# A two-table dense stage: the last token tile's weights kept in two parts, the first of which is given back at key 80

## The chip, the cores and the metric

The kernel runs on one core of a Trainium2 chip. The metric is device time of one execution in microseconds (us). Engines are named as the profile names them: PE multiplies matrices, ACT (ScalarE) copies and evaluates functions, DVE (VectorE) and POOL (GpSimd) work elementwise, SP issues most DMAs, POOL issues the indirect ones (gathers).

## The reference

Two transformer blocks over 512 tokens of width 1024, then a final norm. The change lies in the last part of the second block, a PEER layer: each token picks, for 8 heads, 16 of 128 x 128 experts, each of them one row of a table u and one row of a table v.

```python
def chunk(xc):
    ...
    eidx = jnp.take_along_axis(cidx, pos, axis=-1)
    g = jax.nn.softmax(best, axis=-1)
    a = jnp.einsum('chkd,cd->chk', u_tab[eidx], xc)
    wgt = (jax.nn.gelu(a.astype(jnp.float32)) * g).astype(xc.dtype)
    return jnp.einsum('chk,chkd->cd', wgt, v_tab[eidx])
```

## The kernel before

The function `peer` holds the layer. The tokens stand in four tiles of 128. Three of them (384 tokens, `TD`) are computed densely: for every one of the 128 first keys (here "a key", 128 experts) the kernel multiplies all tokens by the u chunk, takes gelu, multiplies by the tokens' weights for these experts (zero for experts not picked) and multiplies the result by the v chunk, all 128 keys summed in PSUM (`yp`). The fourth tile is computed sparsely: 128 gathers of u rows and 128 of v rows (`grow`), one expert of each of the 128 tokens at a time, with the products made on DVE (`gy` sums the v rows).

Each f32 chunk of a table (128 x 1024, 512 KB) is split for PE into a high and a low half: `wload` loads it into `wraw` (4 buffers, shared by all loads), ACT copies the high half (L69: `whi`, or `vhi`), DVE subtracts (L70: `wlo`, `vlo`). A product takes three matmuls (L87 to L89).

Stages around the change:

- *Weight build* (L1800 on): for each of the three tiles and 32 groups of four tokens, DVE makes one-hot matrices, PE multiplies them into a PSUM bank, and ACT evicts the bank into `gs` (L1820), a tile of 128 x 128 keys x 128 tokens, 64 KB a partition. Between the groups, first-table chunks of keys below 80 (`AHEAD`) and u gathers are worked off. After tiles 0 and 1 `gs` is stored to HBM in four parts (`gd`); tile 2's weights stay in SBUF.
- *Dense stage, keys 0 to 79*: the first-table results lie in HBM (`ad`) and are loaded. `v_prep` loads the other tiles' weights (`gw`), loads and splits the v chunk (a pool `vs` of its own with two buffers each of `vhi` and `vlo`, except for keys 0 to 3, 126 and 127), POOL multiplies weights and gelu (L1851 for two tiles, L1852 for the third out of `gs`), ACT and DVE split the product (`wah`, `wal`), and `v_mm` issues 18 matmuls into `yp`.
- *Dense stage, keys 80 to 123*: in addition `u_chunk` of the next key: load, split, 24 matmuls into `acc`, gelu on ACT (L1596, `ga`).
- Keys 124 to 127 and the final norm.

After each key `gather` is called with a count so that all 256 gathers are out by key 121: 80 are made before the dense stage, 59 in keys 0 to 79, 117 in keys 80 to 121, two or three a key. A gather takes a `grow` buffer (4 of them); right after it `use(lag)` works off rows until only `lag` are outstanding, 3 in the dense stage.

Order: POOL's instructions, and DVE's in the loop over keys, run in the order of the program text. The other engines' orders, SP's too, are fixed at build time by the framework's own estimate of when things become ready. Every engine and queue then runs its list strictly in order. A buffer's next user waits for the last reader of the one before; a pool opened where a closed one lay waits for the readers of the tiles that it covers.

Of the kernel before, what the change touches and what calls it, by code (L numbers as in the profile page):

```python
# [9 lines left out]
F32 = mybir.dt.float32  # L10
# [5 lines left out]
AF = mybir.ActivationFunctionType  # L16
ALU = mybir.AluOpType
# [4 lines left out]
D = 1024  # L22
# [24 lines left out]
class Emit:  # L47
# [1514 lines left out]
    def peer(self):  # L1562
        tc, nc, A = self.tc, self.nc, self.A
# [5 lines left out]
        gd = [tc.dram_tile([ND - 1, 128, 32, 128], F32, name=f"gd{j}") for j in range(4)]  # L1569
        ad = tc.dram_tile([AHEAD, 128, TD], F32, name="ad")  # L1570
        xd = tc.dram_tile([S, D], F32, name="xd")
        with ExitStack() as es:
# [15 lines left out]
            def u_chunk(c, eng=None):  # L1588

                wh, wl = self.wload(A["puT"][c], eng=eng)  # L1590
                p = self.acc()
                for k in range(KD):
                    s_ = slice(k * 128, k * 128 + 128)
                    self.mm3(p[:, :TD], wh[:, s_], wl[:, s_], hh[:, k, :TD], hl[:, k, :TD], k == 0, k == KD - 1)
                g = dn.tile([128, TD], F32, name="ga", bufs=4)
                nc.scalar.activation(g, p[:, :TD], AF.Gelu_apprx_tanh)  # L1596
                if c < AHEAD:
                    self.dma(ad[c], g)
                    return None
                return g  # L1600

            def ahead(n, eng=nc.gpsimd):
                for _ in range(n):
                    if nu[0] < AHEAD:
                        u_chunk(nu[0], eng)
                        nu[0] += 1
# [28 lines left out]
            ga = es.enter_context(tc.tile_pool(name="gat", bufs=4, side="right"))  # L1635
            er = es.enter_context(ExitStack())
# [2 lines left out]

            es.enter_context(tc.manual_schedule(engines={mybir.EngineType.Pool}))  # L1640

            ng, rows = [0], []

            def gather(n, lag=2):


                for _ in range(n):
                    i = ng[0]
                    if i == 256:
                        return  # L1650
                    ng[0] += 1
                    s = i % 128
                    if i == 128:
                        use(0)
                        self.dma(ht, A["g_fin"].to_broadcast([128, D]))
                        nc.scalar.activation(wt, at, AF.Gelu_apprx_tanh)
                        nc.gpsimd.tensor_tensor(wt, wt, gg, op=ALU.mult)
                    r = ga.tile([128, D], F32, name="grow")
                    nc.gpsimd.indirect_dma_start(out=r, out_offset=None, in_=A["pu" if i < 128 else "pvr"],  # L1659
                                                 in_offset=bass.IndirectOffsetOnAxis(ap=ei[:, s:s + 1], axis=0))  # L1660
                    rows.append((i, r))
                    use(lag)

            def use(lag):
                while len(rows) > lag:
                    i, r = rows.pop(0)
                    s = i % 128
                    if i < GPOOL:
                        nc.gpsimd.tensor_tensor(r, r, ht, op=ALU.mult)
                        nc.scalar.activation(r, r, AF.Copy, accum_out=at[:, s:s + 1])  # L1670
                    elif i < 128:
                        stt(r, r, 1.0, ht, op0=ALU.mult, op1=ALU.mult, accum_out=at[:, s:s + 1])  # L1672
                    elif s == 0:
                        ts(gy, r, wt[:, 0:1], None, op0=ALU.mult)
                    else:
                        stt(gy, r, wt[:, s:s + 1], gy, op0=ALU.mult, op1=ALU.add)  # L1676
# [3 lines left out]
            with ExitStack() as ek:  # L1680
# [98 lines left out]
                for t in range(ND):  # L1779
                    c = slice(t * 32, t * 32 + 32)  # L1780
                    p = self.bank()
# [9 lines left out]

            ev = es.enter_context(ExitStack())
            pg = ev.enter_context(tc.tile_pool(name="pg", bufs=1))
            gs = pg.tile([128, 128, 128], F32, name="gs")
            with ExitStack() as ek:
                p2 = ek.enter_context(tc.tile_pool(name="pg2", bufs=2))
                spare = self.wr.rearrange("p k e -> p (k e)")
                i1 = spare[:, 0:128]
                nc.gpsimd.iota(i1, pattern=[[1, 128]], base=0, channel_multiplier=0,
                               allow_small_or_imprecise_dtypes=True)  # L1800
                ih = spare[:, 128:192].bitcast(F16).rearrange("p (a b) -> p a b", b=2)
                nc.vector.tensor_copy(spare[:, 128:192].bitcast(F16), i1)
                nu0, ng0 = nu[0], ng[0]
                for t in range(ND):
                    for q in range(32):

                        e = eT[:, t * 32 + q].rearrange("p j n i -> p (j n) i")
                        o = p2.tile([128, 8, 64, 2], F16, name="oh", bufs=3)
                        tt(o, ih[:, None].to_broadcast([128, 8, 64, 2]),
                           e[:, 0:8, None].to_broadcast([128, 8, 64, 2]), op=ALU.is_equal)  # L1810
                        w = p2.tile([128, 8, 64, 2], F16, name="ohw", bufs=3)
                        for j in range(2):
                            tt(w[:, 4 * j:4 * j + 4], o[:, 4:8],  # L1813
                               e[:, 8 + 4 * j:12 + 4 * j, None].to_broadcast([128, 4, 64, 2]), op=ALU.mult)
                        p = self.bank()
                        for i in range(4):
                            for j in range(2):
                                mm(p[:, i * 128:i * 128 + 128], lhsT=o[:, i].rearrange("p a b -> p (a b)"),  # L1818
                                   rhs=w[:, 4 * j + i].rearrange("p a b -> p (a b)"), start=j == 0, stop=j == 1)
                        nc.scalar.activation(gs[:, :, q * 4:q * 4 + 4], p.rearrange("p (t e) -> p e t", t=4), AF.Copy,  # L1820
                                             scale=1.0 / WSCALE)
                        n = 32 * t + q + 1
                        ahead(nu0 + (AHEAD - nu0) * n // (32 * ND) - nu[0], None)
                        gather(ng0 + GH * n // (32 * ND) - ng[0], 3)
                    if t < ND - 1:
                        for j in range(4):
                            self.dma(gd[j][t], gs[:, j * 32:j * 32 + 32])
                ahead(AHEAD)

            er.close()  # L1830
            vs = ev.enter_context(tc.tile_pool(name="vs", bufs=2))
            eb.close()
            py = es.enter_context(tc.tile_pool(name="py", bufs=1, space=PSUM))
            yp = [py.tile([128, 512], F32, name=f"yp{i}") for i in range(2 * ND)]
            TG = TD - 128

            def v_prep(c, g, ah=None, al=None):

                if g is None:
                    g = dn.tile([128, TD], F32, name="ga", bufs=4)  # L1840
                    self.dma(g, ad[c])
                gw = dn.tile([128, TD], F32, name="gw", bufs=4)
                self.dma(gw[:, :TG], gd[c // 32][:, :, c % 32].rearrange("t a n -> a t n"))
                if c < 4 or c >= 126:
                    wh, wl = self.wload(A["pv"][c])
                else:
                    w = self.wraw.tile([128, 1024], F32, name="wraw")
                    self.dma(w, A["pv"][c])
                    wh, wl = vs.tile([128, 1024], F32R, name="vhi"), vs.tile([128, 1024], F32R, name="vlo")
                    self.split(wh, wl, w)  # L1850
                nc.gpsimd.tensor_tensor(gw[:, :TG], gw[:, :TG], g[:, :TG], op=ALU.mult)  # L1851
                nc.gpsimd.tensor_tensor(gw[:, TG:], gs[:, c], g[:, TG:], op=ALU.mult)  # L1852
                if ah is None:
                    ah, al = dn.tile([128, TD], F32R, name="wah"), dn.tile([128, TD], F32R, name="wal")
                self.split(ah, al, gw)
                return c, ah, al, wh, wl
# [11 lines left out]
            em.enter_context(tc.manual_schedule(engines={mybir.EngineType.DVE}))  # L1868
            g = None
            for c in range(124):  # L1870
                ng_ = u_chunk(c + 1) if AHEAD <= c + 1 < 128 else None
                v = v_prep(c, g)
                for t in range(ND):
                    v_mm(v, t)
                g = ng_
                if c < AHEAD:
                    m = 256 - left + n0 * (c + 1) // AHEAD
                else:
                    m = 256 - left + n0 + (left - n0) * min(c + 1 - AHEAD, GLAST - AHEAD) // (GLAST - AHEAD)
                gather(m - ng[0], 3)  # L1880
            use(0)

            gl = [g] + [u_chunk(c) for c in (125, 126, 127)]
# [43 lines left out]
AHEAD = 80  # L1927
# [15 lines left out]
WSCALE = 2.0 ** 14  # L1943
# [169 lines left out]
```

## Time and profile before

| what | us |
|---|---|
| median of 3 runs (lowest, highest) | 2685.59 (2677.74, 2690.04) |
| the profiled execution | 2691.68 |
| its span, first to last instruction | 2689.6 |
| busy: PE, DVE, ACT, POOL | 2435.8, 1819.5, 1084.8, 940.5 |

The profile is of one execution; times in its rows count from the span's start. In a row of the timeline or of the groups, the text in brackets or behind the bar is the idle time of the engine before the instruction and what ended it. The weight build lies at about 1607 to 1895 us, keys 0 to 79 end at about 2236, key 123 begins at 2636.61.

### The profile page before, as it was taken

Reading aid. Unit: us, or ns where it says so; the run is one execution under the profiler, and the core shown is the slowest. Engines: PE = TensorE matmul, PEld = TensorE weight load, DVE = VectorE, ACT = ScalarE, POOL = GpSimd, SP = SyncE. Lnnn points to the kernel's source line nnn. Section 1 sums busy time; section 2 is a strip of 40 time slices with the busy share of each in tenths; the row PEclk is TensorE's granted clock in tenths of the full one; section 3 lists DMA queues with packets and bytes.
Section 4 is the critical chain, followed back from the end, with each engine's and each line's share of the span. In section 5 each row is a group of like instructions: output and inputs, shape, how many; then the busy total and the mean of one; then the engine's idle time right before and its main releaser. Section 6 shows DMA issues by size and latency. Waiting matters only on the chain. (4 is left out here: it accounts for less than half of the span.)

```text
span 2689.6 us, 33407 instructions
## 1 busy us (share of the span) xinstructions
PE 2435.8 (91%) x11697; PEld 1904.9 (71%) x11697; DVE 1819.5 (68%) x3150; ACT 1084.8 (40%) x1697; POOL 940.5 (35%) x781
## 2 busy tenths in 40 slices
PE   7999888899969978899898989999999999999997
PEld 6776566334427756678687779988788878888886
DVE  6677975364435665654458899977777766767676
ACT  5455434232234235653435554434333333333233
POOL 1001640121100310000056664411677665656661
PEclk9999998899989988999899999999899999999999
DMA  3114675899983311124234459996699987888884
GB/s 144 56 62 155 227 279 206 314 367 409 402 315 115 94 55 32 44 75 156 83 128 135 148 175 329 350 351 248 221 307 302 305 289 256 288 273 298 273 299 139
DMA packets 214782, 585.28 MB, mean 218 GB/s; under 512 B 30437, under 2 KB 85221, under 8 KB 213588
## 3 DMA queue, kind: packets, MB, share of 16 engines
q1 hardware_dynamic: 169684, 429.71, 45.5%
q0 software_dynamic: 44928, 153.42, 16.2%
q8 instruction: 92, 1.51, 0.2%
q14 instruction: 78, 0.64, 0.1%
HBM read 537.65 MB, written 53.78 MB: 220 GB/s over the span
## 5 line engine op out<-in xcount | busy, mean ns | idle before, releaser
L69 ACT ACTIVATE whi<-wraw 128x1024 fp32r<-128x1024 f32 (+1 forms) x280 | 289.1, 1033 | 511.7 <-PE acc L88 191.9
L87 PE MATMUL acc<-hph,whi 128*128 128x384 f32 (+1 forms) x1152 | 404.8, 352 | 23.4 <-ACT ga L1596 21.8
L89 PE MATMUL acc<-hph,wlo 128*128 128x384 f32 (+1 forms) x1152 | 402.7, 350 | 11.4 <-DVE wlo L70 8.2
L88 PE MATMUL acc<-hpl,whi 128*128 128x384 f32 (+1 forms) x1152 | 399.6, 347 | 0.0
L70 DVE TENSOR_TENSOR wlo<-wraw,whi 128x1024 fp32r<-128x1024 f32 (+1 forms) x236 | 288.5, 1223 | 159.1 <-ACT whi L69 157.5
L87 PE MATMUL yp<-vhi,wah 128*128 128x512 f32 x732 | 231.7, 396 | 20.3 <-ACT wah L69 20.3
L87 PEld LDWEIGHTS acc<-hph,whi 128*128 128x128 f32 x1152 | 220.5, 192 | 35.4 <-ACT ga L1596 26.3
L89 PEld LDWEIGHTS acc<-hph,wlo 128*128 128x128 f32 x1152 | 220.2, 191 | 25.1 <-DVE wlo L70 15.3
L88 PE MATMUL yp<-vlo,wah 128*128 128x512 f32 x732 | 231.4, 395 | 0.0
L89 PE MATMUL yp<-vhi,wal 128*128 128x512 f32 x732 | 228.2, 395 | 0.0
L88 PEld LDWEIGHTS acc<-hpl,whi 128*128 128x128 f32 x1152 | 220.6, 191 | 7.5 <-DVE hpl L70 0.5
L1851 POOL TENSOR_TENSOR gw<-gw,ga 128x256 f32<-128x256 f32 x128 | 172.3, 1346 | 147.8 <-DMA ga<-ad 77.2
L1659 POOL DMA_INDIRECT grow<-pu,ei x128 | 150.9, 1179 | 206.5 <-DVE grow L1672 170.5
L70 DVE TENSOR_TENSOR vlo<-wraw,vhi 128x1024 fp32r<-128x1024 f32 x122 | 160.1, 1312 | 92.9 <-ACT vhi L69 92.8
L1659 POOL DMA_INDIRECT grow<-pvr,ei x128 | 173.2, 1353 | 123.5 <-DVE gy L1676 95.1
L69 ACT ACTIVATE wah<-gw 128x384 fp32r<-128x384 f32 x126 | 66.0, 524 | 279.4 <-POOL gw L1852 223.0
L87 PEld LDWEIGHTS yp<-vhi,wah 128*128 128x128 f32 x732 | 139.7, 191 | 52.0 <-ACT wah L69 24.1
L1676 DVE SCALAR_TENSOR_TENSOR gy<-grow,wt,gy 128x1024 f32<-128x1024 f32 x127 | 164.0, 1291 | 16.2 <-DMA grow<-pvr,ei 14.1
L70 DVE TENSOR_TENSOR wal<-gw,wah 128x384 fp32r<-128x384 f32 x126 | 93.8, 745 | 114.9 <-ACT wah L69 114.8
L89 PEld LDWEIGHTS yp<-vhi,wal 128*128 128x128 f32 x732 | 139.2, 190 | 31.7 <-DVE wal L70 2.4
L88 PEld LDWEIGHTS yp<-vlo,wah 128*128 128x128 f32 x732 | 139.8, 191 | 28.2
L70 POOL TENSOR_TENSOR wlo<-wraw,whi 128x1024 fp32r<-128x1024 f32 x44 | 106.1, 2416 | 152.5 <-ACT whi L69 139.2
(702 smaller groups left out, 5178.9 us busy)
## 6 DMA issues: line engine op xcount, KB each, us to landing
wraw<-wgu SPq DMA_DIRECT2D x128, 512.0 KB
wraw<-puT SPq DMA_DIRECT2D x128, 512.0 KB
wraw<-pv SPq DMA_DIRECT2D x128, 512.0 KB
wraw<-wd SPq DMA_DIRECT2D x64, 512.0 KB
aw<-wada SPq DMA_DIRECT2D x48, 512.0 KB
gd<-gs SPq DMA_DIRECT2D x8, 2048.0 KB
gw<-gd SPq DMA_DIRECT2D x128, 128.0 KB
ad<-ga SPq DMA_DIRECT2D x80, 192.0 KB
```

The source lines that it names most:

```text
L69: nc.scalar.activation(hi, src, AF.Copy)
L70: (eng or nc.vector).tensor_tensor(lo, src, f32(hi), op=ALU.subtract)
L87: mm(ps, lhsT=wh, rhs=xh, start=first, stop=False)
L88: mm(ps, lhsT=wh, rhs=xl, start=False, stop=False)
L89: mm(ps, lhsT=wl, rhs=xh, start=False, stop=last)
L1659: nc.gpsimd.indirect_dma_start(out=r, out_offset=None, in_=A["pu" if i < 128 else "pvr"], in_offset=bass.IndirectOffsetOnAxis(ap=ei[:, s:s ...
L1676: stt(gy, r, wt[:, s:s + 1], gy, op0=ALU.mult, op1=ALU.add)
L1851: nc.gpsimd.tensor_tensor(gw[:, :TG], gw[:, :TG], g[:, :TG], op=ALU.mult)
```

## The change

`gs` becomes two tiles: `ga_` with keys 0 to 79 (40 KB a partition, on the right side of SBUF, in the pool group `er`) and `gb` with keys 80 to 127 (24 KB). Each eviction becomes two instructions, and the stores of tiles 0 and 1 are cut at key 80. At key 80 `er` is closed, and a new pool `vs` is opened in its place, with three buffers `vraw` for loads of the second table, two of `vhi` and of `vlo`, and three more row buffers `grow2`; from then on the lag is 6, and three of each seven rows go to `grow2`. Keys below 80 take the shared `wload`.

```diff
-            ng, rows = [0], []
+            ng, rows, more = [0], [], []
...
-                    r = ga.tile([128, D], F32, name="grow")
+                    r = more[0].tile([128, D], F32, name="grow2", bufs=3) if more and (i - more[1]) % 7 < 3 else \
+                        ga.tile([128, D], F32, name="grow")
...
-            gs = pg.tile([128, 128, 128], F32, name="gs")
+            gb = pg.tile([128, 128 - AHEAD, 128], F32, name="gsb")
+            ga_ = er.enter_context(tc.tile_pool(name="pga", bufs=1, side="right")).tile([128, AHEAD, 128], F32, name="gsa")
+            gsp = (ga_, 0, AHEAD), (gb, AHEAD, 128)
...
-                        nc.scalar.activation(gs[:, :, q * 4:q * 4 + 4], p.rearrange("p (t e) -> p e t", t=4), AF.Copy,
-                                             scale=1.0 / WSCALE)
+                        pe = p.rearrange("p (t e) -> p e t", t=4)
+                        for g_, lo, up in gsp:
+                            nc.scalar.activation(g_[:, :, q * 4:q * 4 + 4], pe[:, lo:up], AF.Copy, scale=1.0 / WSCALE)
...
-                            self.dma(gd[j][t], gs[:, j * 32:j * 32 + 32])
+                            for g_, lo, up in gsp:
+                                lo_, up_ = max(lo, j * 32), min(up, j * 32 + 32)
+                                if lo_ < up_:
+                                    self.dma(gd[j][t][:, lo_ - j * 32:up_ - j * 32], g_[:, lo_ - lo:up_ - lo])
...
-            er.close()
-            vs = ev.enter_context(tc.tile_pool(name="vs", bufs=2))
+            vs = None
...
-                if c < 4 or c >= 126:
+                if c < AHEAD or c >= 126:
                     wh, wl = self.wload(A["pv"][c])
                 else:
-                    w = self.wraw.tile([128, 1024], F32, name="wraw")
+                    w = vs.tile([128, 1024], F32, name="vraw", bufs=3)
...
-                nc.gpsimd.tensor_tensor(gw[:, TG:], gs[:, c], g[:, TG:], op=ALU.mult)
+                gt = ga_[:, c] if c < AHEAD else gb[:, c - AHEAD]
+                nc.gpsimd.tensor_tensor(gw[:, TG:], gt, g[:, TG:], op=ALU.mult)
...
             for c in range(124):
+                if c == AHEAD:
+                    er.close()
+                    vs = ev.enter_context(tc.tile_pool(name="vs", bufs=2, side="right"))
+                    more += [vs, ng[0]]
...
-                gather(m - ng[0], 3)
+                gather(m - ng[0], 6 if more else 3)
```

## Rows read from the trace of the kernel before

**Rows 1.** Windows: us; busy PE, PEld, DVE, ACT, POOL (count); clock, DMA share, GB/s.

```profile
1607.00:1895.00 288.00, 270.41 (x1947) 251.47 (x1947) 253.30 (x460) 125.13 (x201) 101.43 (x65) 0.95 0.83 302
1950.00:2150.00 200.00, 200.00 (x884) 165.65 (x883) 147.59 (x171) 75.21 (x98) 141.84 (x135) 1.00 0.92 305
2277.47:2636.61 359.14, 336.91 (x1639) 297.38 (x1638) 247.95 (x223) 112.70 (x156) 220.76 (x183) 0.98 0.83 285
```

**Rows 2.** Timeline of PE (start, us, instruction, idle before): first matmuls of second-table passes.

```profile
2232.00 0.50 PE L87 MATMUL yp<-vhi,wah 128*128 128x512 f32 x1 [0.43 <-ACT wah L69]
...
2277.47 0.39 PE L87 MATMUL yp<-vhi,wah 128*128 128x512 f32 x1
...
2285.78 0.39 PE L87 MATMUL yp<-vhi,wah 128*128 128x512 f32 x1
...
2319.56 0.39 PE L87 MATMUL yp<-vhi,wah 128*128 128x512 f32 x1
...
2331.93 0.79 PE L87 MATMUL yp<-vhi,wah 128*128 128x512 f32 x1 [3.92 <-ACT wah L69]
...
2636.61 0.50 PE L87 MATMUL yp<-vhi,wah 128*128 128x512 f32 x1 [0.50 <-ACT wah L69]
```

**Rows 3.** Waits, 2277.47 to 2636.61: us in total, times, longest.

```profile
ACT whi L69 <- DMA wraw<-puT: 148.9, 39, 7.7
...
POOL gw L1851 <- issue: 38.2, 28, 9.3
...
PE yp L87 <- ACT wah L69: 15.5, 7, 3.9
DVE gy L1676 <- DMA grow<-pvr,ei: 13.0, 16, 1.6
...
PE acc L89 <- DVE wlo L70: 6.0, 11, 1.3
```

**Rows 4.** Timeline of DVE, SP and ACT, key 90.

```profile
2322.24 1.22 DVE L70 TENSOR_TENSOR wlo<-wraw,whi 128x1024 fp32r<-128x1024 f32 x1
...
2323.49 0.33 SPq L55 DMA_DIRECT2D wraw<-puT  x1
...
2330.41 1.06 ACT L69 ACTIVATE whi<-wraw 128x1024 fp32r<-128x1024 f32 x1 [7.66 <-DMA wraw<-puT]
2331.37 0.51 ACT L69 ACTIVATE wah<-gw 128x384 fp32r<-128x384 f32 x1
```

**Rows 5.** Timeline of DVE, remainders (wal) that bound keys 83 and 88.

```profile
2267.96 0.56 DVE L70 TENSOR_TENSOR wal<-gw,wah 128x384 fp32r<-128x384 f32 x1 [0.91 <-ACT wah L69]
...
2276.09 0.56 DVE L70 TENSOR_TENSOR wal<-gw,wah 128x384 fp32r<-128x384 f32 x1 [0.91 <-ACT wah L69]
...
2310.01 0.56 DVE L70 TENSOR_TENSOR wal<-gw,wah 128x384 fp32r<-128x384 f32 x1 [1.61 <-ACT wah L69]
...
2319.25 0.56 DVE L70 TENSOR_TENSOR wal<-gw,wah 128x384 fp32r<-128x384 f32 x1 [2.58 <-ACT wah L69]
```

**Rows 6.** Timeline of DVE after key 123; waits of PE from 2636 us.

```profile
2637.07 3.92 DVE L1676 SCALAR_TENSOR_TENSOR gy<-grow,wt,gy 128x1024 f32<-128x1024 f32 x3
...
PE yp L87 <- ACT hph L69: 4.0, 1, 4.0
```

**Rows 7.** Timeline of POOL at key 79.

```profile
2230.25 0.72 POOL L1851 TENSOR_TENSOR gw<-gw,ga 128x256 f32<-128x256 f32 x1 [11.32 <-DMA ga<-ad]
2230.94 0.46 POOL L1852 TENSOR_TENSOR gw<-gs,ga 128x128 f32<-128x128 f32 x1
```

**Rows 8.** Groups by shape of ACT in the weight build: count, busy, mean ns, idle before.

```profile
L1820 ACT ACTIVATE gs<-bank 128x512 f32<-128x512 f32 x96 | 53.7, 606 | 58.6 <-PE bank L1818 39.5 <-DMA gd<-gs 13.2 <-issue 5.4
L69 ACT ACTIVATE whi<-wraw 128x1024 fp32r<-128x1024 f32 x50 | 53.3, 1067 | 101.7 <-PE acc L88 101.6
L1596 ACT ACTIVATE ga<-acc 128x384 f32<-128x384 f32 x50 | 23.9, 478 | 4.8 <-issue 4.8
```

**Rows 9.** Timeline of ACT at the end of the build's first tile.

```profile
1771.02 4.03 ACT L1820 ACTIVATE gs<-bank 128x512 f32<-128x512 f32 x8 [13.16 <-DMA gd<-gs]
```

## The prediction

> **What bounds the kernel now.** I read the windows by stage first: they show for each stretch whether PE is full. From 1950 to 2150, within the first 80 keys of the dense stage, PE is busy 200.00 of 200 us, so nothing that helps other engines can pay there. In the stretch from key 84 to key 123 it is busy 336.91 of 359.14 us at a granted clock of 0.98, with the DMA engines at 0.83 [rows 1]. That stretch is where both tables are multiplied in each key, and only there is something to win.
>
> How much, the timeline of PE says. A key there is 24 matmuls of the first table and 18 of the second. Where PE waits for nothing, the second-table pass of key 84 begins at 2277.47 and that of key 85 at 2285.78: 8.31 us. Over the five keys to 2319.56 it is 8.42 us each. From 2277.47 to key 123 at 2636.61 it is 359.14/39 = 9.21 us [rows 2]. So 0.90 us a key, 35 us in all, lie above the bare PE time.
>
> Then the waits of that stretch, to see what takes it: PE waits 15.5 us for the high half of the weights (wah, ACT) and 6.0 us for the low half of a first-table chunk (DVE); the rest is matmuls at the lower clock level after such pauses, 336.91 - 39 x 8.31 = 12.8 us [rows 1, 3]. Behind them stands ACT, which waits 148.9 us for the load of the first table, 39 times, longest 7.7 us [rows 3]. Key 90 shows the mechanism: ACT has the copy of a later first-table chunk ahead of wah in its order; that chunk's load was issued at 2323.49, right behind the DVE subtraction that freed its buffer (2322.24 + 1.22), and came 6.9 us later; wah, whose input was long ready, ran at 2331.37, and PE started at 2331.93 [rows 2, 4]. The load is late because its buffer is: four wraw buffers serve two loads a key, so a load can only be issued two keys ahead of its use.
>
> **The change part by part.**
>
> 1. Loads of the second table from key 80 get three buffers of their own; the four wraw buffers serve the first table alone. A first-table load then follows the subtraction of four keys before, not two: two keys, 16.8 us at 8.42, earlier than the 6.9 us that key 90's load took [rows 2, 4]. A second-table load follows the one of three keys before. I take ACT's 148.9 us to fall to nearly nothing, and with them the late wah. POOL's multiply waits 38.2 us in 28 pieces for nothing that the profile names ("issue") [rows 3]; it needs the gelu of the chunk, which ACT makes behind the late copy, so I count these with them.
> What is late next: the loop DVE to POOL to ACT to DVE. POOL issues a key's second gather only when DVE has used up the row that sat in its buffer, the weight multiplies stand behind the gathers on POOL, wah behind them, and DVE's own next step behind wah. This coupling stays: with seven buffers and a lag of six, the buffer that a gather needs is still freed by the use emitted just before it. Its length without a late load is 8.13 us at key 83 (2267.96 to 2276.09, three rows) [rows 5], under PE's 8.31. So PE sets the pace. Ends: 8.31 (no waits, as in the first 80 keys) and 9.21 (nothing gained). I take 8.42, the five clean keys, as they have the same work: (9.21 - 8.42) x 39 = -30.8 us.
>
> 2. Three more row buffers and a lag of six. DVE waits 13.0 us in 16 waits for rows that have not landed [rows 3]; with two keys more of flight time these go. They lie inside the 9.21 and are not counted again. At the end six rows instead of three are left for DVE: 3 x 1.31 = 3.9 us, from the three at 2637.07 [rows 6]. PE then still has most of two passes to do; a wait of 4.0 us for ACT in the tail may shrink with earlier loads [rows 6]. Ends -4.0 and +3.9; I take +1.
>
> 3. Keys below 80 split their weights into the shared ring of three instead of a ring of two. PE is full there, 200.00 of 200 us [rows 1], and hides it: 0. Without that cover a third buffer could only shorten waits of ACT, so the sign would be a gain.
>
> 4. The hand-over at key 80. The new pool lies on the first part, so the second-table load of key 80 stands on SP until POOL has done its multiply of key 79 (2230.94 + 0.46), and the loads behind it on SP stand too; DVE's and ACT's work of key 80 waits for it. From there: 6.9 us of load, 1.06 of copy, 1.22 of subtraction [rows 4, 7], 9.2 us. PE has meanwhile wah and its remainder (about 1.1), the second-table pass of key 79 and a first-table pass, together 8.31: 9.4 us. So just hidden. Now the five keys from 2232.00 to 2277.47 take 45.47 us [rows 2], 3.4 more than 5 x 8.42, after POOL waited 11.32 us for a stored gelu row that SP had issued late [rows 7]. Ends: -3.4 and +9.2 (nothing hidden); I take 0, since one pays for the other.
>
> 5. Each of 96 evictions of the weight build becomes two, of 320 and 192 elements. No row has these shapes. Together they take no less than one of 512 (0.606) and no more than two of 384 (0.478 each): 0 to 0.35 us more, 0 to 34 us of ACT. Between the rows of 512 and 1024 (1.067) the line has a fixed part of 0.145 [rows 8]; I take that, 14 us of ACT. ACT is busy 125.13 of 288 us there [rows 1] and waits 101.6 us for PE [rows 8], so it hides, except where ACT catches up: at a tile's end it stood 13.16 us behind the stores and then ran 8 evictions in a row while PE lacked banks [rows 9]. Two such places x 8 x 0.145 = +2 us. The Trainium skill (ScalarE: Activation LUTs, "What ACT_TABLE_LOAD costs") gives 186 ns plus 0.833 ns an element, an estimate of 0.19 us a split and so +3 us here; no run here has shown it yet.
>
> 6. The stores of the weights become ten instead of eight, of the same bytes; the last of them ends the wait of the second half at the same time as now. Two issues more on SP: 0, with the 14 us of waiting above as cover.
>
> Sum: -30.8 + 1 + 0 + 0 + 2 = -27.8 us. The profiled execution took 2691.68 us, so 2663.9; it lies 6.1 above the median of the runs, 2685.59, and on that scale the forecast is **2658 us**. Best ends together: -35.1 - 4.0 - 3.4 = -42.5, 2643.
>
> **The rivals.**
>
> *The loop of DVE and POOL takes over.* With all rows landed, DVE runs the three row updates back to back, and POOL's gathers fit worse between them. Key 88 shows it: no late load, three updates in a row, and 9.24 us from 2310.01 to 2319.25 [rows 5]. Against it stands key 83, also three in a row, at 8.13 [rows 5], and that the mean of 9.21 holds all the late loads as well: if a key of three rows took 9.24 without them, the mean would lie above that. 117 rows in 42 keys make about 30 of these 39 keys keys of three rows; with 9.24 there and 8.42 in the other nine it is 9.05 a key: -6 + 3 = -3, 2683 us. Chance 0.12. The Trainium skill (Advanced Engine Details and Errata, "GPSIMD Details") says that POOL shares a read and a write interface with DVE and conflicts with DVE instructions that have two SBUF inputs, as these updates have; by that rule 9.05, by the row of key 83 8.42. The trace agrees in part, at key 88 and not at key 83.
>
> *The DMA engines become the bound.* At 8.42 us a key they need 285 x 9.21/8.42 = 312 GB/s and a share of 0.91. The first 80 keys run at 305 and 0.92 with PE full [rows 1], which speaks against it; that these have more small transfers speaks neither way. If the rate stays at 295, between the two rows, a key takes 8.90: -12 + 3, 2677 us. Chance 0.11.
>
> *Slower: ACT runs ahead into PE.* With loads early, the copy of a first-table chunk no longer waits for its load but for PE to free its buffer, as in the build, 101.6 us [rows 8]. Should it stand ahead of wah in ACT's order, each key's wah starts only when a first-table pass has ended, and PE waits in every key as it did at key 90: 0.56 from wah's start to PE's [rows 2, 4], and per wait 12.8/18 = 0.71 of slower matmuls [rows 1, 3]. That is 8.42 + 1.27 = 9.69 a key, +19 + 3, 2707 us. It decides from 0.79 us a key. For it speaks that this order occurred, at key 90; against it that in the clean keys, where loads came in time, PE never waited for wah [rows 2]. Chance 0.09.
>
> *The change does not do what it says.* SP issues in one order; if a first-table load stands there behind a load whose buffer comes free late, it goes out no earlier, and a key stays at 9.21: +3, 2689 us. Chance 0.06.
>
> **How the numbers follow.** The forecast has 0.62, with a range of its own of 2640 to 2671: all waits gone at the low end, 8.76 a key at the high end. A measurement of this kernel can tell about 0.5%, 13.4 us, from no change: faster is below 2672, slower above 2699. Faster: 0.62 and a third of the DMA case, 0.66; slower 0.09; the rest, 0.25, the same. The range runs from 2640 to 2683, which takes in the loop and the DMA case and leaves out the last two rivals (0.15) and 0.03 below.
>
> **What would show it.** Right: between keys 84 and 123 ACT's waits for the first table's load near zero, POOL's "issue" waits shorter, DVE's waits for rows gone, second-table passes 8.3 to 8.5 us apart at clock 1.00; evictions of 0.7 to 0.8 us a pair; the first 80 keys unchanged. Wrong: wah still late with ACT waiting for PE (the slower rival), POOL's gathers as the last thing before wah in keys of 9 us (the loop), loads issued early but landing late (DMA), or loads issued no earlier.

## The result and the profile after

The changed kernel takes 2649.24 us in the median (2638.58 to 2652.60), the kernel before beside it 2685.28: a ratio of 0.9857, 95% interval 0.9833 to 0.9880, so 1.4% faster. The forecast was 2658 in a range of 2640 to 2683.

The profiled execution took 2638.58 us, 10.7 below its median, and the one before lay 6.1 above its own; stages are therefore compared with two more profiled executions of the changed kernel (table below), and whole times by ratios.

Windows of the changed kernel, the three stages of [rows 1] and the end (us; busy PE, PEld, DVE, ACT, POOL with counts; clock, DMA share, GB/s):

```profile
1607.00:1890.00 283.00, 268.75 (x1938) 249.84 (x1938) 253.11 (x460) 131.02 (x292) 103.01 (x64) 0.95 0.85 307
1950.00:2150.00 200.00, 200.00 (x884) 165.59 (x883) 154.92 (x171) 72.32 (x99) 147.58 (x135) 1.00 0.89 304
2264.37:2590.41 326.04, 326.04 (x1639) 294.01 (x1639) 243.23 (x224) 118.06 (x156) 181.57 (x182) 1.00 0.90 310
2590.41:2636.90 46.49, 33.55 (x163) 29.20 (x162) 32.46 (x66) 17.64 (x35) 7.57 (x8) 0.91 0.29 102
```

The third line is the result in short. Keys 84 to 123 take 326.04 us instead of 359.14, PE is busy in all of them and its clock stays at the upper level. That is 8.36 us a key, and the timeline of PE shows it from the first key (it answers to [rows 2]):

```profile
2264.37 0.39 PE L87 MATMUL yp<-vhi,wah 128*128 128x512 f32 x1
...
2272.73 0.39 PE L87 MATMUL yp<-vhi,wah 128*128 128x512 f32 x1
...
2281.09 0.39 PE L87 MATMUL yp<-vhi,wah 128*128 128x512 f32 x1
...
2590.41 0.39 PE L87 MATMUL yp<-vhi,wah 128*128 128x512 f32 x1
```

Waits of the same stretch, all engines, the six longest of ten lines (us in total, times, longest; answers to [rows 3]):

```profile
ACT whi L69 <- PE acc L88: 114.0, 39, 2.9
DVE wal L70 <- ACT wah L69: 76.8, 38, 5.0
POOL gw L1859 <- issue: 68.9, 38, 7.2
POOL grow L1661 <- DVE gy L1678: 54.9, 36, 3.0
ACT wah L69 <- POOL gw L1861: 52.5, 39, 2.2
ACT vhi L69 <- PE yp L89: 41.4, 39, 1.1
```

In none of the ten is PE the waiting engine, none has DVE waiting for rows, and in none does the copy `whi` wait for its load: the 148.9 us in 39 waits of [rows 3] have become 114.0 us in 39 waits for PE. Who waits for whom has turned round. ACT, DVE and POOL now wait for the bottleneck, which is what a stage at its bound looks like; that these waits are long costs nothing.

Where the time went, by stage, from the first matmuls of PE's passes in the timeline (us; "changed" is three profiled executions of the changed kernel):

| stage | before | changed |
|---|---|---|
| weight build, first matmul to key 0's second-table pass | 288.66 | 285.60, 288.64, 289.11 |
| key 66 to key 70 | 20.62 | 18.22, 18.23, 18.22 |
| key 78 to key 84 | 55.54 | 51.32, 51.35, 51.32 |
| key 84 to key 123 | 359.14 | 326.04, 326.04, 326.04 |
| key 123 to the last DVE instruction (below: the end) | 49.88 | 43.40, 43.40, 43.40 |

The build varies by 3.5 us between executions of the changed kernel, and the keys 0 to 66, not in the table, by 2.5, so neither shows an effect of the change. The other four stages agree to 0.03 us, and they are 46.2 us shorter: 33.1 in the keys 84 to 123, 6.5 in the end, 4.2 around key 80 and 2.4 around key 67.

That is more than the 36 us between the medians, and the likely reason is the column "before": it is one execution, 6.1 us above its median. Its key 0 begins at 1896.38 us, among those of the changed kernel (1892.78, 1896.55, 1902.12), so its excess lies behind that, in the dense stage. f_evict_only (below) bears this out. From key 60 on its instructions stand in the order of before on every engine, and its time is that of before (ratio 1.0000), but its profiled execution has 356.30 for the keys 84 to 123 and 45.83 for the end. So where a kernel has waits, these two stages differ by up to 4 us without any edit to them; single differences of that size below show no cause.

### The profile page after: what moved, and what is told of

The parts are those of the page before. It is cut to its first block, busy times and chain, and to the rows that moved or that the text cites. A ratio compares the mean times of both kernels' runs of the same rounds, so it can differ in the third digit from the quotient of the medians.

```text
span 2636.9 us, 33511 instructions
## 1 busy us (share of the span) xinstructions
PE 2414.6 (92%) x11697; PEld 1894.9 (72%) x11697; DVE 1827.0 (69%) x3150; ACT 1093.2 (41%) x1793; POOL 914.7 (35%) x781
## 5 line engine op out<-in xcount | busy, mean ns | idle before, releaser
L69 ACT ACTIVATE whi<-wraw 128x1024 fp32r<-128x1024 f32 (+1 forms) x356 | 368.6, 1036 | 466.5 <-PE acc L88 303.4
L70 DVE TENSOR_TENSOR wlo<-wraw,whi 128x1024 fp32r<-128x1024 f32 (+1 forms) x312 | 395.8, 1269 | 163.2 <-ACT whi L69 161.2
L1859 POOL TENSOR_TENSOR gw<-gw,ga 128x256 f32<-128x256 f32 x128 | 135.8, 1061 | 174.7 <-issue 85.6
L87 PE MATMUL yp<-whi,wah 128*128 128x512 f32 x480 | 185.1, 390 | 3.2 <-ACT wah L69 3.2
L88 PE MATMUL yp<-wlo,wah 128*128 128x512 f32 x480 | 185.6, 389 | 0.0
L89 PE MATMUL yp<-whi,wal 128*128 128x512 f32 x480 | 159.3, 389 | 0.0
L1674 DVE SCALAR_TENSOR_TENSOR grow<-grow,htok 128x1024 f32<-128x1024 f32 x112 | 157.3, 1408 | 0.4 <-DMA grow<-pu,ei 0.2
L728 PE MATMUL bank<-wraw,st 128*64 128x512 f32 x512 | 142.5, 603 | 0.9 <-DVE act L734 0.9
L87 PE MATMUL acc<-xh,whi 128*128 128x512 f32 x288 | 116.3, 404 | 3.0 <-DVE hn_o L199 3.0
L89 PE MATMUL acc<-xh,wlo 128*128 128x512 f32 x288 | 115.0, 400 | 3.4 <-DVE wlo L70 3.4
```

The source lines that it names most:

```text
L69: nc.scalar.activation(hi, src, AF.Copy)
L70: (eng or nc.vector).tensor_tensor(lo, src, f32(hi), op=ALU.subtract)
L87: mm(ps, lhsT=wh, rhs=xh, start=first, stop=False)
L88: mm(ps, lhsT=wh, rhs=xl, start=False, stop=False)
L89: mm(ps, lhsT=wl, rhs=xh, start=False, stop=last)
L728: mm(p[r], lhsT=st[:, k, r], rhs=ws[s][:, kk * 512:kk * 512 + 512], start=k == 0, stop=k == KD - 1)
```

## The experiments

Each kernel is a short edit of one of the two. The stages of their profiled executions, one each, stand in one table:

| kernel | time, us | ratio to before (95%) | 66 to 70 | 78 to 84 | 84 to 123 | 123 to end |
|---|---|---|---|---|---|---|
| a_loads_only | 2646.75 | 0.9842 (0.9822 to 0.9863) | 18.21 | 51.35 | 326.04 | 42.22 |
| b_rows_only | 2670.76 | 0.9943 (0.9925 to 0.9961) | 18.22 | 51.35 | 352.05 | 45.20 |
| c_split_only | 2675.46 | 0.9952 (0.9934 to 0.9970) | 18.22 | 51.34 | 352.42 | 46.32 |
| d_again | 2647.99 | 0.9852 (0.9833 to 0.9871) | 18.23 | 51.35 | 326.04 | 43.40 |
| e_ring3_only | 2679.59 | 0.9982 (0.9971 to 0.9993) | 18.22 | 53.23 | 349.94 | 49.61 |
| f_evict_only | 2684.17 | 1.0000 (0.9987 to 1.0012) | 20.66 | 56.15 | 356.30 | 45.83 |
| g_one_vraw | 2664.04 | 0.9920 (0.9895 to 0.9946) | 18.22 | 51.36 | 337.37 | 46.68 |
| h_hoist | 2643.57 | 0.9846 (0.9818 to 0.9873) | 18.22 | 50.02 | 326.04 | 42.20 |
| i_two_vraw | 2643.71 | 0.9848 (0.9822 to 0.9875) | 18.22 | 51.36 | 326.04 | 42.22 |
| j_shared_six | 2645.16 | 0.9845 (0.9818 to 0.9872) | 18.22 | 52.41 | 326.47 | 42.30 |
| k_best | 2641.22 | 0.9835 (0.9811 to 0.9858) | 16.32 | 50.02 | 326.03 | 42.22 |
| l_after_again | 2647.96 | 0.9857 (0.9834 to 0.9881) | 18.22 | 51.32 | 326.04 | 43.40 |

**Which part pays.** Four kernels on one chip: the change without the rows, without the load buffers, without both, and whole.

a_loads_only:

```diff
-                    more += [vs, ng[0]]
+                    pass
-                gather(m - ng[0], 6 if more else 3)
+                gather(m - ng[0], 3)
```

> The changed kernel with its three buffers for loads of the second table, but without the three more row buffers and with a lag of 3. If late table loads alone made the loss (the prediction's first step), a key from 84 to 123 takes 8.36 to 8.5 us as in the changed kernel and the ratio to the kernel before is about 0.987. If late rows alone made it, a key stays at 9.1 to 9.2 and the ratio at 0.998 to 1.00. If each of the two holds a key up by itself, DVE waits for rows in most keys and a key takes 8.7 to 9.1.

b_rows_only:

```diff
-                    w = vs.tile([128, 1024], F32, name="vraw", bufs=3)
+                    w = self.wraw.tile([128, 1024], F32, name="wraw")
```

> The changed kernel with three more row buffers and the lag of 6, but the loads of the second table from key 80 go through the shared four buffers again. If late table loads made the loss, ACT waits some 150 us for the first table's loads as before, a key takes 9.0 to 9.2 us and the ratio is 0.995 to 1.00. If late rows made it, a key takes 8.4 to 8.5 and the ratio is about 0.987.

c_split_only has the edits of a and of b together.

> The weights in two parts, the first given back at key 80, but nothing new put into the space: shared load buffers, four row buffers, lag 3. It prices the split evictions and the hand-over. Prediction: evictions cost +2 us, the hand-over 0, a key 9.2 us: ratio 1.00 to 1.002. Rival: the split eviction lets ACT begin before all stores are out and so gains 3 to 6 us in the build: ratio 0.997 to 0.999. If the shared ring of three for the weights of keys below 80 matters, more than that.

d_again is the changed kernel, unaltered.

> The changed kernel once more, with the instructions in the same order on every engine. Its profiled execution lay 10 us under the median of its runs; a second profile tells what of the stage times is the program's and what the execution's. Keys 84 to 123 at 8.36 us again if that stage is paced by PE alone; the 10 us then lie before the weight build. Ratio 0.983 to 0.988.

The load buffers pay: a against c is 0.9842 against 0.9952, some 29 us. In the profiled executions 26.4 of that lie in keys 84 to 123 and 4.1 in the end. The rows pay nothing: b's interval overlaps c's, and a without the rows is not slower than d with them. What the rows did is to be seen in the waits: in a DVE waits for rows as before,

```profile
DVE gy L1678 <- DMA grow<-pvr,ei: 12.5, 17, 1.7
```

and in the changed kernel it doesn't (no such line above); PE's 326.04 us are the same. Once the loads are early, such waits are not on the path. At the end the rows cost 1.2 us (43.40 against 42.22).

In b and c the old stall is back: waits of c in its keys 84 to 123 (148.9 and 15.5 us in before, [rows 3]), and the stretch itself,

```profile
ACT whi L69 <- DMA wraw<-puT: 136.3, 36, 5.8
...
PE yp L87 <- ACT wah L69: 11.8, 7, 2.7
```

```profile
2271.96:2624.38 352.42, 335.20 (x1639) 293.48 (x1639) 246.99 (x222) 112.81 (x156) 216.20 (x183) 1.00 0.85 289
```

The first profiled execution of the changed kernel had been 10 us short of its median, and d was expected to show these 10 us ahead of the weight build. That missed: of the 6.3 us between the two executions 0.7 lie there, 3.0 in the build and 2.5 in the keys 0 to 66.

The miss of the prediction is c. It has neither buffers nor rows, and is 0.48% faster than before, some 13 us, where the prediction's steps 3 to 6 make +2. Key 67, key 80 and the stretch after it were all shorter. Two kernels try to take it apart.

**Where c's gain comes from.** e_ring3_only, of the kernel before:

```diff
-                if c < 4 or c >= 126:
+                if c < AHEAD or c >= 126:
```

> The kernel before with one edit: keys 4 to 79 take their second-table weights from the shared ring of three (as keys 0 to 3 do). No split of the last tile's weights, no new load buffers, no hand-over. The split-and-hand-over kernel had been 12 us faster than before where the prediction had +2, with 2.4 us of it around key 67, 4.2 around key 80 and 6.7 between keys 84 and 123. Theory A, the ring: a third pair of weight buffers below key 80 lets ACT run further ahead and is the cause; then this kernel shows 18.2 us from key 66 to 70 (before: 20.62), 51.3 from key 78 to 84 (before: 55.54), and 2672 to 2678 us in all. Theory B, the split: the shorter evictions (or the order that the framework makes from them) are the cause; then 20.6 and 55.5 stay and the time is 2685 within 4. The prediction's step 3 (nothing, because PE is full there) also says 2685.

f_evict_only, of the kernel before, both tiles in the old pool:

```diff
-            gs = pg.tile([128, 128, 128], F32, name="gs")
+            gb = pg.tile([128, 128 - AHEAD, 128], F32, name="gsb")
+            ga_ = pg.tile([128, AHEAD, 128], F32, name="gsa")
+            gsp = (ga_, 0, AHEAD), (gb, AHEAD, 128)
...
-                        nc.scalar.activation(gs[:, :, q * 4:q * 4 + 4], p.rearrange("p (t e) -> p e t", t=4), AF.Copy,
-                                             scale=1.0 / WSCALE)
+                        pe = p.rearrange("p (t e) -> p e t", t=4)
+                        for g_, lo, up in gsp:
+                            nc.scalar.activation(g_[:, :, q * 4:q * 4 + 4], pe[:, lo:up], AF.Copy, scale=1.0 / WSCALE)
```

(with the stores cut and POOL's multiply reading the two tiles, as in the change)

> The kernel before with one edit: the last tile's weights in two tiles, each eviction in two instructions and the stores cut at key 80, both tiles kept to the end; the ring of two below key 80, the old load buffers and no hand-over. Prediction's step 5: the build 2 us longer and nothing else, 2687. Theory B, the split as cause of the 12 us: 2672 to 2678. Theory A, the ring as cause: no gain, 2685 to 2688. In the build I expect the pair of evictions at 0.78 us (0.443 and 0.337) as in the changed kernel, against 0.606, and the first matmul of the build to the first second-table matmul at 288 within 2 us.

The split of the evictions alone changes nothing that can be told (1.0000, 0.9987 to 1.0012, so within 3 us). The ring of three alone gives 0.18%, about 5 us: less than theory A had, and with 53.23 instead of 51.3 around key 80, but with the 18.22 at key 67 that it named. e's stages are 14.2 us shorter than those of before, 9.2 of them in the keys 84 to 123, which the ratio doesn't bear out; part of these 9.2 is the one execution of before, and what the ring gives there is not told. Key 67 can be followed in the rows. There the gathers change from the first table to the second, and POOL multiplies the sparse weights (`wt`) before the first of these; that product waits for ACT's gelu, and this for DVE's last row. The weight multiplies of the key stand behind it on POOL, wah behind these, and PE behind wah. Timeline of POOL and PE, before:

```profile
2171.11 1.03 POOL L1657 TENSOR_TENSOR wt<-wt,gg 128x128 f32<-128x128 f32 x1 [9.69 <-ACT wt L1656]
...
2175.04 0.79 PE L87 MATMUL yp<-vhi,wah 128*128 128x512 f32 x1 [2.50 <-ACT wah L69]
2175.63 0.63 PE L88 MATMUL yp<-vlo,wah 128*128 128x512 f32 x1
```

and with the ring of three (e_ring3_only):

```profile
2172.14 0.46 POOL L1657 TENSOR_TENSOR wt<-wt,gg 128x128 f32<-128x128 f32 x1 [9.98 <-ACT wt L1656]
...
2176.45 0.50 PE L87 MATMUL yp<-whi,wah 128*128 128x512 f32 x1 [1.61 <-ACT wah L69]
2176.79 0.40 PE L88 MATMUL yp<-wlo,wah 128*128 128x512 f32 x1
```

Counted from PE's key 66 (2168.30 and 2170.61), that multiply runs at 2.81 before and at 1.53 in e: with a third weight buffer it stands 1.28 us earlier against PE, and the pause shrinks by 0.89. The stage shrinks by 2.40; most of the rest is the clock, below.

The remaining 0.30% between e and c, some 8 us (their intervals, from different chips, just miss each other), is not explained by a part: the split alone gives none of it. c's keys 78 to 84 are 1.9 us shorter than e's and its end 3.3, its keys 84 to 123 2.5 longer, which makes 2.7. From key 60 on the two kernels have the same order on every engine except on ACT around key 80, where c makes two second-table copies later; only the 1.9 us lie there. What makes the rest stays open.

**How deep the loads must stand.** Both kernels without the extra rows.

g_one_vraw:

```diff
-                    w = vs.tile([128, 1024], F32, name="vraw", bufs=3)
+                    w = vs.tile([128, 1024], F32, name="vraw", bufs=1)
```

> The changed kernel without the extra rows (2646.8 us), and one load buffer for the second table instead of three. Theory: what paid is that the four old buffers serve the first table alone; one second-table load needs a key's copy (1.06), subtraction (1.22) and load (4 to 5.5 us), together 6.5 to 8 of the 8.36 us of a key, so one buffer just holds the pace: 8.4 to 8.5 a key between keys 84 and 123, 2645 to 2653 us. Rival: each load must be issued two keys ahead as before; then the copy of the second-table chunk comes late in most keys and a key takes 8.8 or more, 2662 us or more.

The theory fell; the rival's time came out (2664.04), though a key takes 8.65 us and not its 8.8. The long wait of ACT has changed its table, at nearly its old size, and what PE waits for is the first table's low half, which DVE makes behind the late second-table chunk (PEld is PE's weight load; waits of g, keys 84 to 123):

```profile
ACT vhi L69 <- DMA vraw<-pv: 138.2, 33, 6.1
...
PEld acc L89 <- DVE wlo L70: 11.2, 20, 0.9
...
PE acc L89 <- DVE wlo L70: 4.9, 11, 0.6
```

The timelines of DVE, SP and ACT at one key show the loop at its longest: the load goes out the moment the subtraction frees the only buffer, and the copy runs 7.7 us later. In the median of the 39 keys it is 6.0, at the least 3.8, where the theory had 4 to 5.5.

```profile
2330.01 1.22 DVE L70 TENSOR_TENSOR vlo<-vraw,vhi 128x1024 fp32r<-128x1024 f32 x1
...
2331.26 0.33 SPq L55 DMA_DIRECT2D vraw<-pv  x1
...
2338.96 1.06 ACT L69 ACTIVATE vhi<-vraw 128x1024 fp32r<-128x1024 f32 x1 [5.87 <-DMA vraw<-pv]
...
2340.05 1.22 DVE L70 TENSOR_TENSOR vlo<-vraw,vhi 128x1024 fp32r<-128x1024 f32 x1 [0.63 <-ACT vhi L69]
```

Key 90 of before had 6.9 us for the load of a same-sized chunk [rows 4]; the lower figure leaned on the hand-over, where a copy started 3.9 us after its load went out. From load to freed buffer it is 10.0 us here (2331.26 to the end of the next subtraction at 2341.27) and 8.6 in the median, more than the 8.36 of a key.

i_two_vraw: as g, with `bufs=2`.

> The changed kernel without the extra rows, and two load buffers for the second table (three: 8.36 us a key between keys 84 and 123; one: 8.65, with 138 us of ACT's waits for that load). Theory: what a load needs is to be issued more than one key before its copy; with two buffers it follows the subtraction of two keys before, some 14 us ahead of a load that lands in 4 to 7 us, so 8.36 to 8.40 a key and 2647 us. Rival: any ring shorter than three keys lets some loads come late: 8.5 a key or more, 2652 us or more.

Two buffers of its own are enough for the second table, beside four for the first: 326.04 us, and ACT waits for no load in these keys.

j_shared_six:

```diff
+                if more:
+                    w = more[0].tile([128, 1024], F32, name="vraw", bufs=6)
+                    self.dma(w, A["puT"][c])
...
-                    w = vs.tile([128, 1024], F32, name="vraw", bufs=3)
+                    w = vs.tile([128, 1024], F32, name="vraw", bufs=6)
```

> From key 80 on both tables load through one ring of six buffers in the space that was given back (the four old ones idle), without the extra rows. Theory, depth: a load was late because its buffer was; with six buffers for two loads a key each is issued three keys ahead, and it makes no difference that the tables share the ring: 8.36 to 8.42 a key between keys 84 and 123, 2647 us. Rival, separation: in a shared ring a first-table load waits for the subtraction of a second-table chunk that stands late in the order; then some of the stalls at keys 90, 95, 99 and on remain, 8.6 a key or more, 2656 us or more.

Six shared buffers give 326.47 us, as good as four and three apart. So what the four shared ones of before lack is depth, and a table needs no buffers of its own once there are six. The timelines of SP and PE have the lead: from the issue of a first-table load to the first matmul on its chunk it is 17.1 us in before (the median of these keys), 26.5 with six shared buffers and 37.1 in the changed kernel: two keys, three, and over four. But six shared are nearer to the edge. Loads of the first table are waited for again, 80.1 us in all, and PE idles for 0.13 us:

```profile
ACT whi L69 <- DMA vraw<-puT: 80.1, 27, 4.2
```

```profile
2279.76:2606.23 326.47, 326.34 (x1639) 293.99 (x1639) 260.08 (x225) 114.18 (x156) 225.32 (x183) 1.00 0.91 311
```

So the same line of the waits stands for 22 us of PE in before (359.14 - 336.91, [rows 1]) and for 0.13 here. Its size doesn't tell; whether PE waits at the end of that chain does. What tells ahead of time is how long wah lies ready before PE takes it: over the 39 keys at the least 0.05 us in before, 1.5 with six shared buffers and 4.2 in the changed kernel.

**What is left at keys 67 and 79.** h_hoist, without the extra rows:

```diff
+                if c == AHEAD - 2:
+                    gn = dn.tile([128, TD], F32, name="ga", bufs=4)
+                    self.dma(gn, ad[c + 1])
+                if c == AHEAD - 1:
+                    g = gn
                 ng_ = u_chunk(c + 1) if AHEAD <= c + 1 < 128 else None
```

> The changed kernel without the extra rows (2646.8 us), and the stored gelu row of key 79 loaded one key earlier in the program text. It stood on SP behind a first-table load that waited 3.1 us for its buffer, and POOL waited 10.9 us for it. Theory: PE's key 79 takes 10.2 us only because of that row; with it 8.4, so 1.9 us less from key 78 to 84 (51.35 to 49.5), and the whole is 2645 us. Rival: the load of key 80's second-table chunk, which waits for POOL's last read of the first part, becomes what is late, and the 51.35 stays. In total time the two can hardly be told apart; the stretch in the profile tells.

The stretch falls by 1.33 us to 50.02, six keys at 8.34, less than the 1.9 forecast. The one pause of PE in it, 1.00 us in the changed kernel, is gone. So what had remained of the hand-over was not the new pool but the late gelu row of key 79, as in before [rows 7]. The changed kernel, POOL and SP (the row waits on SP behind two loads that stand for 3.46 us):

```profile
2220.20 0.74 POOL L1859 TENSOR_TENSOR gw<-gw,ga 128x256 f32<-128x256 f32 x1 [11.00 <-DMA ga<-ad]
2220.90 0.46 POOL L1861 TENSOR_TENSOR gw<-gsa,ga 128x128 f32<-128x128 f32 x1
```

```profile
2212.47 3.46 SPq L55 DMA_DIRECT2D wraw<-puT  x2
2215.97 0.43 SPq L55 DMA_DIRECT2D ga<-ad  x1
2221.39 1.28 SPq L55 DMA_DIRECT2D vraw<-pv  x3
```

k_best adds to h:

```diff
-                        nc.scalar.activation(wt, at, AF.Gelu_apprx_tanh)
-                        nc.gpsimd.tensor_tensor(wt, wt, gg, op=ALU.mult)
+                    if i == 131:
+                        nc.scalar.activation(wt, at, AF.Gelu_apprx_tanh)
+                        nc.gpsimd.tensor_tensor(wt, wt, gg, op=ALU.mult)
```

> The changed kernel without the extra rows, with the gelu row of key 79 loaded a key earlier, and with the gelu of the sparse tile's weights and its product on POOL made three gathers later, ahead of their first use instead of ahead of the first gather of the second table. That product stood on POOL for 9.7 us at key 67, in front of the weight multiplies of that key. Theory: the pause of PE at key 67 came from it: 16.3 to 16.5 us from key 66 to 70 instead of 18.2, and 50.0 from key 78 to 84 as in the run with the earlier row alone; 2642 us. Rival: another wait, of DVE for the last rows of the first table, ends the same pause, and 18.2 stays: 2644 us.

l_after_again, in the same rounds, is the changed kernel.

> The changed kernel once more, in the same rounds as the best version: 2647 to 2650 us, so the best version should be 5 to 7 us faster, some 0.2%, at the edge of what five rounds can tell.

The multiply no longer waits (first row, POOL), and PE has no pause from key 66 to 70 (second fence, window):

```profile
2175.49 0.46 POOL L1658 TENSOR_TENSOR wt<-wt,gg 128x128 f32<-128x128 f32 x1
```

```profile
2167.55:2183.87 16.32, 16.32 (x73) 13.51 (x72) 11.64 (x12) 6.10 (x9) 11.59 (x13) 1.00 0.84 287
```

16.32 instead of 18.22: the product on POOL was the cause. k took 2636.77 to 2644.30 us in five runs, the changed kernel 2644.38 to 2650.01 in the same rounds: 6.7 us in the medians, more than the 4.4 that the stages show (1.9, 1.3 and 1.2). The two intervals against before overlap, the runs themselves do not. It has the lowest median of all; from h and i (0.9846 and 0.9848 against 0.9835) it can't be told apart in total time.

## Why the prediction was right, and where it was not

**Step 1 (own buffers, -30.8) held.** The stage lost 33.1 us against the one execution of before; a against c gives 29 in all. The mechanism is the one described: late loads gone, and with them late copies and late wah. The period is 8.36, PE's own, where 8.42 was taken. One part of the account was wrong: the lower clock was to explain why PE was busy longer in before. Its busy time did fall, by 10.9 us (336.91 to 326.04), but c is busy for 335.20 at a granted clock of 1.00 (its window above), so the clock alone does not account for it; what else lengthens the matmuls of c was not shown. That POOL's "issue" waits would shrink was wrong: they grew from 38.2 to 68.9 us. POOL's multiply runs when ACT's gelu is done (ACT ends it at 2315.99, POOL starts at 2316.13, rows below), and that gelu now keeps PE's time.

**Step 2 (rows, +1) held**: +1.2 in the end, nothing in the loop. The end as a whole became 6.5 us shorter than in the one execution of before, which the sum didn't have. The executions of c and f have 3.6 and 4.1 of that without buffers or rows, and f even with the order of before, so up to 4 us are no effect of the change that could be told. a against c has 4.1 at the end, and the wait of 4.0 us for ACT in the tail [rows 6], 3.2 in c, is gone in a and in the changed kernel; it is gone in b too, where loads are late, so early loads are not its only cure.

**Step 3 (ring of three, 0) failed.** The sentence "PE is full there" rested on a window from 1950 to 2150, which [rows 1] show rightly; the pause at key 67 lies at 2172 to 2175, outside it. A cover was read from a part of the stage and claimed for the whole. The ring gave -2.4 at key 67 and 2.3 of the 4.2 around key 80 (e_ring3_only); the sign was the one that the step named for a stretch without cover.

**Step 4 (hand-over, 0) came out beyond its low end.** Its five keys, 79 to 83, went from 45.47 us to 41.09, -4.4 where the low end was -3.4; 2.5 of that come with the ring of three alone (42.99 in e_ring3_only). The chain was as told, and SP issues the loads at 2221.39, the instant POOL's last read ends (rows of h_hoist's part); but the first copy came 3.9 us after, not 6.9:

```profile
2225.28 1.06 ACT L69 ACTIVATE vhi<-vraw 128x1024 fp32r<-128x1024 f32 x1 [0.35 <-DMA vraw<-pv]
```

With copy and subtraction that makes 6.2 us under the 9.4 of cover, so nothing was left uncovered to set against the shorter stretch.

**Step 5 (evictions, +2) had the price of a pair nearly right, and no loss can be told.** Groups of ACT in the build, changed kernel:

```profile
L1827 ACT ACTIVATE gsa<-bank 128x320 f32<-128x320 f32 x96 | 41.2, 443 | 52.5 <-PE bank L1823 45.2 <-DMA gd<-gsa 5.0 <-issue 1.6
L1827 ACT ACTIVATE gsb<-bank 128x192 f32<-128x192 f32 x96 | 31.0, 337 | 9.3 <-DMA gd<-gsb 9.3
```

0.443 + 0.337 against 0.606 is 0.174 a pair; the line through the wider rows gave 0.145. The Trainium skill's formula (ScalarE: Activation LUTs, "What ACT_TABLE_LOAD costs") gave 0.19, a little nearer. The +2 was for tile ends, where ACT had evicted eight banks in a row behind the stores. It now starts with the first part while the second still goes out:

```profile
1761.18 2.09 ACT L1827 ACTIVATE gsa<-bank 128x320 f32<-128x320 f32 x6 [4.95 <-DMA gd<-gsa]
1768.77 1.45 ACT L1827 ACTIVATE gsb<-bank 128x192 f32<-128x192 f32 x6 [5.50 <-DMA gd<-gsb]
```

Of the burst of 4.03 us behind the last store [rows 9], 1.45 is left there. f shows the net, 1.0000, within 3 us. Step 6, the stores, lies inside that.

**The rivals.** *The DMA engines*: 310 GB/s at a share of 0.90 with PE full, against the 295 that this rival needed; out. *The loop of DVE and POOL*: keys with three updates in a row take 8.36 us, not 9.24. The gathers do get slower beside them, 1.86 us within DVE's three updates against 0.98 just ahead of them; the Trainium skill's rule (Advanced Engine Details and Errata, "GPSIMD Details") agrees with that beside the updates, but not in every row: the third gather takes 1.01 us beside the subtraction wlo, which has two SBUF inputs as well. A key's three gathers still fit. In key 88 of before the second gather began only at 2313.51, after 2.96 us of waiting for DVE, and it and the third took 1.71 and 1.97 us; the weight multiply stood right behind them, at 2317.51. In key 91 of the changed kernel (below) the second begins at 2311.54, and the multiply waits for the gelu, no longer for the gathers. What moved the gathers was not tested by itself. *ACT runs ahead into PE*: its condition came true, in every key. The copy of the first-table chunk waits for PE, 114.0 us in all, and stands ahead of wah. Its price did not. Timelines of ACT, POOL and DVE of the changed kernel, key 91:

```profile
2314.56 1.06 ACT L69 ACTIVATE whi<-wraw 128x1024 fp32r<-128x1024 f32 x1 [2.92 <-PE acc L88]
2315.52 0.47 ACT L1596 ACTIVATE ga<-acc 128x384 f32<-128x384 f32 x1
2317.32 0.53 ACT L69 ACTIVATE wah<-gw 128x384 fp32r<-128x384 f32 x1 [1.32 <-POOL gw L1861]
```

```profile
2309.08 0.98 POOL L1661 DMA_INDIRECT grow<-pvr,ei  x1
2311.54 1.86 POOL L1661 DMA_INDIRECT grow<-pvr,ei  x1 [1.48 <-DVE gy L1678]
2313.71 1.01 POOL L1661 DMA_INDIRECT grow<-pvr,ei  x1 [0.30 <-DMA vraw<-pv]
2316.13 0.74 POOL L1859 TENSOR_TENSOR gw<-gw,ga 128x256 f32<-128x256 f32 x1 [1.41 <-issue]
```

```profile
2309.99 3.92 DVE L1678 SCALAR_TENSOR_TENSOR gy<-grow,wt,gy 128x1024 f32<-128x1024 f32 x3
2313.83 1.22 DVE L70 TENSOR_TENSOR wlo<-wraw,whi 128x1024 fp32r<-128x1024 f32 x1
```

wah ends at 2317.85, and PE takes it at 2322.89 (seven periods after 2264.37), 5.0 us later: between the first-table pass that frees the buffer and the second-table pass that needs this wah PE has two more passes. Over the 39 keys it is 4.2 us or more. The rival priced the wait as if wah were needed right away. An order that looks harmful is so only with its deadline beside it.

**The sum** came to -27.8; measured is -36 to -38 (medians; 1.43%). Step 1 came out at its size, some 29 by the ratios; the difference is in steps 3 to 6, which c shows as -13 instead of +2, and of these -13 only the ring's 5 have a cause that was shown; added up by the ratios, -13, -29 and +1 make -41, a few us more than measured, which the intervals leave open.

## What to carry to other kernels

Where a weight load is late because its buffer is, count buffers in keys of lead. Here a buffer's turn-round, load, copy and subtraction, took 8.6 us in the median and up to 10.0 against a key of 8.36: one buffer for the second table stalled and two did not, and of a ring that both tables share four buffers stalled and six did not. Two buffers for each table apart, the depth of before without its sharing, were not run, so at that depth the two stay unseparated. Before an edit is costed at nothing because the bottleneck is full, look at every stretch that the edit touches, not at a clean sample of it. A long wait of an engine off the path is no loss in itself: follow it to the bottleneck, and ask how much time it had to spare there.

## What the runs showed of the hardware

In these rows short pauses of PE cost little more than themselves, longer ones mostly also the clock after them. After 2.50 us at key 67 the granted clock over the next 5 us was 0.68 in before, after 1.61 us it was 1.00 in e_ring3_only; after 3.92 us at key 90 it was 0.73 in before, after 0.41 us 1.00 in c_split_only. The length of the pause does not settle it by itself: after 2.42 us the clock was 1.00 in c_split_only (2405.88 to 2410.88), after 1.83 us it was 0.66 in before (2378.08 to 2383.08). Windows at key 67 of before, then of e:

```profile
2175.04:2180.00 4.96, 4.96 (x15) 3.97 (x16) 4.16 (x3) 0.90 (x2) 4.79 (x6) 0.68 1.01 383
```

```profile
2176.45:2181.45 5.00, 5.00 (x22) 4.15 (x23) 5.00 (x5) 1.64 (x3) 4.82 (x6) 1.00 0.96 335
```

In nearly equal time 22 matmuls run instead of 15. So a pause that shrinks by 0.89 us saved 2.40, and the key's slow matmuls went with it (1.00 is the 2.4 GHz level, the lower one is 1.2 GHz).
